# Layer norm sums on TensorE, its silu on ScalarE, and the third attention branch among the second group's heads

## The chip, the cores and the metric

The kernel runs on one core of one Trainium2 chip. The metric is the device time of one execution in microseconds (us), as the median of several runs. The engines named here are TensorE (PE: matmuls, and PEld for its weight loads), VectorE (DVE), ScalarE (ACT), GpSimd (POOL) and SyncE (SP), which issues the loads of the weights.

## The reference, cut to what matters

A trunk of two layers on 256 tokens of width 2048, in float32. Each layer is a mixer and a gated feed-forward part, each with an RMS norm ahead and a residual sum behind. Only the first layer's mixer is touched: a conv module and a sparse attention read the same input, and their outputs (1024 columns each) go through one output product.

```
def conformer_conv(u, conv_w, conv_b, ln_w, ln_b):
    a, g = split(u, 2)
    h = a * sigmoid(g)
    h = causal_depthwise_conv(h, conv_w, width=31) + conv_b      # 1024 channels
    mu  = mean(h, axis=-1)
    var = mean(square(h - mu), axis=-1)
    hn  = (h - mu) * rsqrt(var + EPS) * ln_w + ln_b
    return silu(hn)

def nsa_attention(q, k_cmp, v_cmp, k_slc, v_slc, k_win, v_win, gates):
    # 16 heads of 64, 4 key groups; three branches a head, each a masked softmax
    o_cmp = softmax(q @ k_cmp - slope * dist) @ v_cmp            # 15 compressed blocks
    o_slc = softmax(q @ k_sel - slope * dist) @ v_sel            # selected blocks
    o_win = softmax(q @ k_win - slope * dist) @ v_win            # window
    return gate0 * o_cmp + gate1 * o_slc + gate2 * o_win

def even_mixer(h, ...):
    u = h @ w_in                        # conv input, q, six key and value inputs, gates
    a_out = conformer_conv(u[conv part], ...)
    b_out = nsa_attention(u[the rest], ...)
    return concatenate([a_out, b_out]) @ w_out
```

## The kernel before

**Tiles.** Features lie on the 128 partitions and the 256 tokens along the free dimension. A float32 value is kept as a high and a low part (`xhl`, `mhl`: a tile of four features blocks by two parts by 256 tokens), and a product with a weight is three matmuls: high by high, low by high, high by low. A weight block comes by a DMA from SyncE's queue into `raw` (L167); ScalarE copies its high part `whi` (L178), and VectorE or GpSimd subtracts the low part `wlo` (L179). The tuple `lo_pool` says which: it is read in turn, and a 1 gives the block to GpSimd. The matmuls of L204 to L206 sum the three products in one PSUM tile `acc`; L229 to L231 do the same for the value inputs.

**Order.** `drive` (L237) takes a list of jobs, each a weight block's worth of output columns in four units, and a list of background steps; it spreads the steps over the units, up to the share `until` of them. A scheduler then sets each engine's order from these priorities; within an engine instructions start in order.

**The mixer's stages** (function `even`). The conv inputs come first (jobs 0 to 7). The conv has 31 taps per channel tile on VectorE (L408 to L411), 8 tiles in four pairs; the running sum of a pair lies in PSUM (`mx`), and the last tap writes the tile of `cy`. The taps are the background of jobs 2 to 7, of the key jobs 8 and 9, the value job, the gate job and the query jobs 12 and 13 of head group 0. Next come jobs 14 and 15 (queries of group 1) and 10 and 11 (the inputs that are compressed, `evac_c`, L529), with the layer norm as background: `ln_steps` (L421 to L479).

**The layer norm before.** GpSimd adds the eight tiles of `cy` to one (L432, L427, L428), TensorE takes the mean over channels with one matmul (L437), ScalarE copies it to SBUF, VectorE subtracts it from both halves of `cy` (L444), ScalarE squares them (L446), GpSimd adds the squares (L450, L427, L428). `inv_rms` (L133) has two matmuls of one column for the sum over partitions (L139), the inverse root on VectorE, a matmul that spreads it over the partitions (L150) and a copy (L152). The product with it is on GpSimd for one half and VectorE for the other (L459), scale and bias are eight VectorE instructions (L461), silu is a sigmoid on ScalarE (L468) and a product on GpSimd (L469), and then the halves are parted into `mhl` (L475 high, L476 low), which the output product's matmuls read.

**Output product and attention.** `out_jobs(0, 8)` multiplies the conv's eight tiles by the first half of `w_out`; its background is the compression of keys and values (`compress_steps`; its block sums are L628 on GpSimd), the heads of group 0 (`attn[0][0]`: scores, weigh, turn, values) and then group 0's third branch `attn[0][1]`. `out_jobs(8, 12)` needs group 0's output, and has group 1's heads and, behind them, its third branch `attn[1][1]` as background. `out_jobs(12, 16)` needs group 1's output. The third branch has six steps: `cmp_scores` (matmuls L842, copies L850, transposes L855, bias add L858, slope L861), `cmp_exp` (L867 to L869), `cmp_sum` (L874 to L886), `cmp_turn` (transposes L894, copy L897) and two `cmp_values` (matmuls L904, sum L914, and the split into `mhl`).

Of the kernel before, what the change touches and what calls it, by code (L numbers as in the profile page):

```python
# [10 lines left out]
F32 = mybir.dt.float32  # L11
# [57 lines left out]
class Net:  # L69
# [62 lines left out]

    def inv_rms(self, sums, n):  # L133


        nc = self.nc
        ps = self.mx()
        for tb in range(2):
            nc.tensor.matmul(ps[:, tb : tb + 1], sums[:, tb * 128 : tb * 128 + 128], self.ones[:, 0:1], start=True, stop=True)  # L139
        v = self.tile(self.tp, [128, 2], "rs_v", bufs=2)  # L140
        nc.vector.tensor_scalar(v, ps[:, 0:2], 1.0 / n, EPS, op0=ALU.mult, op1=ALU.add)
        tok = self.tile(self.tp, [128, 2], "rs_tok", bufs=2)
        self.rsqrt(tok, v, "rs")
        diag = self.t256("rs_diag", bufs=1)
        for tb in range(2):
            nc.vector.tensor_scalar(
                diag[:, tb * 128 : tb * 128 + 128], self.ca("ident"), tok[:, tb : tb + 1], None, op0=ALU.mult
            )
        pb = self.mx()
        nc.tensor.matmul(pb[:, :S], self.ones, diag, start=True, stop=True)  # L150
        bc = self.t256("rs_bc", bufs=2)
        nc.scalar.copy(bc, pb[:, :S])  # L152
        return tok, bc
# [155 lines left out]
    def norm_done(self):  # L309
        self.tok, self.bc = self.inv_rms(self.ssq, D)  # L310

# [48 lines left out]
    def even(self, xhl, start):  # L360
# [60 lines left out]
        def ln_steps():  # L421
            st = {}
            t4 = lambda tag, dt=F32: self.tile(cv, [128, 4, S], tag, dt)
            w, b = self.cb("lnw"), self.cb("lnb")

            def fold(t):
                nc.gpsimd.tensor_add(t[:, 0:2], t[:, 0:2], t[:, 2:4])  # L427
                nc.gpsimd.tensor_add(t[:, 0], t[:, 0], t[:, 1])  # L428

            def ysum():  # L430
                st["s"] = s = self.quarter("mhl1", (128, 4, S), F32)
                nc.gpsimd.tensor_add(s, cy[:, 0:4], cy[:, 4:8])  # L432
                fold(s)

            def mean():
                pm = self.mx()
                nc.tensor.matmul(pm[:, :S], self.mean1024, st["s"][:, 0], start=True, stop=True)  # L437
                m = self.tile(cv, [128, S], "l_m")
                nc.scalar.copy(m, pm[:, :S])
                st["m"] = m  # L440

            def center(h):
                y = cy[:, 4 * h : 4 * h + 4]
                nc.vector.tensor_sub(y, y, st["m"].unsqueeze(1).to_broadcast([128, 4, S]))  # L444
                q = st[h] = t4("l_q") if h else self.quarter("mhl0", (128, 4, S), F32)
                nc.scalar.activation(q, y, AF.Square)  # L446

            def sqsum():
                q = st[0]
                nc.gpsimd.tensor_add(q, q, st[1])  # L450
                fold(q)

            def var():
                _, st["r"] = self.inv_rms(st[0][:, 0], 1024)

            def out(h):
                y = cy[:, 4 * h : 4 * h + 4]
                eng = nc.vector if h else nc.gpsimd
                eng.tensor_mul(y, y, st["r"].unsqueeze(1).to_broadcast([128, 4, S]))  # L459
                for j in range(4 * h, 4 * h + 4):  # L460
                    nc.vector.tensor_scalar(  # L461
                        cy[:, j], cy[:, j], w[:, j : j + 1], b[:, j : j + 1], op0=ALU.mult, op1=ALU.add
                    )

            def silu(h):
                y = cy[:, 4 * h : 4 * h + 4]
                g = t4("l_q")
                nc.scalar.activation(g, y, AF.Sigmoid)  # L468
                nc.gpsimd.tensor_mul(y, y, g)  # L469

# [7 lines left out]
            two = lambda f: [lambda: f(0), lambda: f(1)]  # L478
            return [ysum, mean] + two(center) + [sqsum, var] + two(out) + two(silu) + two(parts)  # L479

# [46 lines left out]
        def evac_c(kv):  # L527
# [13 lines left out]
        self.raw_size = 2048  # L541
        self.lo_pool = (0, 1, 1)
        self.drive([job(1, evac_a(0))], [lambda: nc.sync.dma_start(self.cst_b, a["cst_b"])], until=0.25)
# [7 lines left out]
            + [job(12 + i, evac_q(0, i)) for i in range(2)],  # L551
            conv,
            until=0.98,
# [3 lines left out]
            [job(14 + i, evac_q(1, i)) for i in range(2)] + [job(10, evac_c(0)), job(11, evac_c(1))],  # L557
            [turn_gates] + ln_steps() + [self.lower_bound],
            until=0.8,
# [32 lines left out]
        heads = attn[0][0]  # L592
        mixed = []
        for i in range(max(len(comp), len(heads))):
            mixed += comp[i : i + 1] + heads[i : i + 1]
        self.drive(out_jobs(0, 8), mixed + attn[0][1] + attn[1][0][:5])
        self.drive(out_jobs(8, 12), attn[1][0][5:] + attn[1][1], until=0.8)
        self.lo_pool = (0,)
# [124 lines left out]
    def nsa(self, P, q4, kt, vt, gt, o):  # L723
# [107 lines left out]
        def cmp_scores():  # L831

            mem = self.quarter("xhl3", (128, 1280), F32)
            z = cs["z"] = mem[:, 0:256].rearrange("p (b h n) -> p b h n", b=2, h=8)
# [504 lines left out]
```

## Time and profile before

| what | value |
|---|---|
| median of 3 runs | 2456.01 us (2455.55 to 2456.85) |
| profiled execution, its own time | 2458.43 us |
| its span in the trace | 2456.2 us |
| TensorE busy | 2396.2 us (98%) |
| VectorE, ScalarE, GpSimd busy | 1543.1, 1171.6, 622.2 us |
| mean granted clock of TensorE | 0.989 of full speed |
| stage of the conv's taps, 62 to 192 us: TensorE, VectorE, GpSimd busy | 129.42, 123.56, 73.42 us of 130 |
| 440 us to the end: TensorE busy | 1999.22 us of 2016 |

The span is what the trace covers; the execution's own time is 2.2 us longer. A row on a wait names the engine and line that waited, then the engine, tile and line that ended the wait. The granted clock is a share of TensorE's full speed; 0.50 is the lower of its two levels (1.2 and 2.4 GHz). Stretches are in us from the span's start.

### The profile page before, as it was taken

How to read it: one execution, taken by the hardware profiler on the slowest of the kernel's cores; microseconds unless marked ns; L12 is line 12 of the kernel's file. 1: busy time of each engine (PE TensorE's matmuls, PEld its weight loads, DVE VectorE, ACT ScalarE, POOL GpSimd, SP SyncE). 2: the span in 40 equal slices, each digit the busy share in tenths (PEclk: the TensorE clock that was granted, in tenths of full speed). 3: DMA queues.
4: the chain of work that ended last, by engine and by line, in shares of the span. 5: the costliest groups of instructions: out<-in, count | busy, mean ns of one | idle time of the engine just before them, and what ended most of it. 6: DMA issues, size and time to landing. Idle time of an engine off the chain costs nothing.

```text
span 2456.2 us, 36598 instructions
## 1 busy us (share of the span) xinstructions
PE 2396.2 (98%) x14532; PEld 2114.6 (86%) x14532; DVE 1543.1 (63%) x2253; ACT 1171.6 (48%) x1728; POOL 622.2 (25%) x586
## 2 busy tenths in 40 slices
PE   7999898999999999999999999999999999999997
PEld 6999877888888888888888888888888888888886
DVE  7997556756555655557656766676655555555554
ACT  4344444645444544455544443355544444444554
POOL 5656522311111121113203223132111111121123
PEclk9999999999999999999999999999999999999998
DMA  5554422655555555555554444445555555555553
GB/s 204 185 169 163 159 72 69 215 189 187 188 187 187 186 179 194 188 183 187 191 180 164 155 155 155 151 158 188 185 187 188 186 188 188 183 191 189 188 183 125
DMA packets 62267, 427.89 MB, mean 174 GB/s; under 512 B 6928, under 2 KB 7056, under 8 KB 15248
## 3 DMA queue, kind: packets, MB, share of 16 engines
q1 hardware_dynamic: 61776, 425.04, 52.2%
q8 instruction: 114, 1.87, 0.3%
q10 hardware_dynamic: 320, 0.52, 0.1%
q14 instruction: 57, 0.47, 0.1%
HBM read 422.91 MB, written 2.10 MB: 173 GB/s over the span
## 4 chain that ended last, share of the span: by engine, by line
PE 94%; DVE 3%; POOL 1%; issue 1%; ACT 0%; DMA 0%; DVEq 0%; SPq 0%; POOLq 0%; ACTq 0%
PE acc L211 44%; PE acc L212 22%; PE acc L204 3%; PE acc L205 3%; PE acc L206 3%; PE acc L209 3%; PE acc L230 2%; PE acc L229 2%; PE acc L231 2%; PE acc L208 2%; PE mx L1071 1%; DVE wlo L179 1%; PE mx L643 1%; PE mx L745 1%; DVE a_z L788 0%
## 5 line engine op out<-in xcount | busy, mean ns | idle before, releaser
L179 DVE TENSOR_TENSOR wlo<-raw,whi 128x1024 fp32r<-128x1024 f32 x754 | 972.1, 1290 | 679.8 <-ACT whi L178 670.0
L178 ACT ACTIVATE whi<-raw 128x1024 fp32r<-128x1024 f32 (+1 forms) x809 | 843.6, 1043 | 915.1 <-PE acc L211 605.4
L211 PE MATMUL acc<-xhl,whi 128*128 128x512 f32 x3120 | 1089.4, 395 | 0.0
L212 PE MATMUL acc<-xhl,wlo 128*128 128x256 f32 x3120 | 844.3, 281 | 0.0
L211 PEld LDWEIGHTS acc<-xhl,whi 128*128 128x128 f32 x3120 | 573.1, 188 | 111.0
L212 PEld LDWEIGHTS acc<-xhl,wlo 128*128 128x128 f32 x3120 | 588.9, 189 | 25.0
L211 PE MATMUL acc<-mhl,whi 128*128 128x512 f32 x1500 | 520.5, 396 | 1.9 <-DVE mhl L120 1.8
L212 PE MATMUL acc<-mhl,wlo 128*128 128x256 f32 x1500 | 398.7, 281 | 0.0
L264 POOL TENSOR_TENSOR e_u<-e_s,rs_bc 128x256 f32<-128x256 f32 x192 | 148.6, 775 | 905.7 <-DVE e_s L257 867.8
L211 PEld LDWEIGHTS acc<-mhl,whi 128*128 128x128 f32 x1500 | 274.0, 188 | 53.5 <-DVE mhl L120 2.0
L212 PEld LDWEIGHTS acc<-mhl,wlo 128*128 128x128 f32 x1500 | 283.2, 189 | 15.5 <-DVE wlo L179 0.2
L278 POOL TENSOR_TENSOR x<-x,e_c 128x256 f32<-128x256 f32 x108 | 109.0, 1022 | 420.2 <-DVE x L277 420.2
L179 POOL TENSOR_TENSOR wlo<-raw,whi 128x1024 fp32r<-128x1024 f32 (+1 forms) x55 | 136.4, 2481 | 132.1 <-ACT whi L178 125.7
L204 PE MATMUL acc<-xhl,whi 128*128 128x256 f32 (+1 forms) x528 | 149.6, 289 | 8.6 <-ACT whi L178 8.6
L206 PE MATMUL acc<-xhl,wlo 128*128 128x256 f32 (+1 forms) x528 | 149.6, 289 | 6.6 <-DVE wlo L179 3.6
L205 PE MATMUL acc<-xhl,whi 128*128 128x256 f32 (+1 forms) x528 | 150.5, 288 | 3.7 <-DVE xhl L1199 3.7
L255 ACT COPY e_c<-acc 128x256 f32<-128x256 f32 x208 | 77.6, 373 | 156.0 <-PE acc L209 155.9
L257 DVE TENSOR_TENSOR e_s<-acc,e_c 128x256 f32<-128x256 f32 x208 | 87.3, 421 | 72.2 <-ACT e_c L255 70.2
L230 PE MATMUL acc<-wlo,xhl 128*128 128x512 f32 x288 | 114.0, 396 | 0.6 <-DVE wlo L179 0.6
L231 PE MATMUL acc<-whi,xhl 128*128 128x512 f32 x288 | 112.5, 391 | 0.0
L204 PEld LDWEIGHTS acc<-xhl,whi 128*128 128x128 f32 (+1 forms) x528 | 102.7, 195 | 8.9 <-ACT whi L178 8.6
L206 PEld LDWEIGHTS acc<-xhl,wlo 128*128 128x128 f32 (+1 forms) x528 | 102.0, 195 | 7.8 <-DVE wlo L179 4.1
(226 smaller groups left out, 2569.8 us busy)
## 6 DMA issues: line engine op xcount, KB each, us to landing
raw<-in_gu SPq DMA_DIRECT2D x176, 1024.0 KB, 5.0
raw<-in_dn SPq DMA_DIRECT2D x64, 1024.0 KB, 5.1
raw<-in_od_fq SPq DMA_DIRECT2D x32, 1024.0 KB, 5.0
raw<-in_od_ig SPq DMA_DIRECT2D x32, 1024.0 KB, 4.8
raw<-in_ev_in SPq DMA_DIRECT2D x30, 1024.0 KB, 5.0
raw<-in_dn SPq DMA_DIRECT2D x32, 768.0 KB, 4.4
raw<-in_od_out SPq DMA_DIRECT2D x16, 1024.0 KB, 5.0
raw<-in_ev_out SPq DMA_DIRECT2D x8, 1024.0 KB, 5.1
```

Source lines behind the costliest of these rows:

```text
L178: nc.scalar.activation(hi[:, :m], rs, AF.Copy)
L179: eng.tensor_sub(lo[:, :m], rs, hi[:, :m].bitcast(F32))
L204: nc.tensor.matmul(o[:, :S], h, a[:, 0, :], start=first, stop=False)
L205: nc.tensor.matmul(o[:, :S], h, a[:, 1, :], start=False, stop=False)
L206: nc.tensor.matmul(o[:, :S], l, a[:, 0, :], start=False, stop=end)
L211: nc.tensor.matmul(o, h, both, start=first, stop=False)
L212: nc.tensor.matmul(o[:, S:], l, a[:, 0, :], start=False, stop=False)
L230: nc.tensor.matmul(o, src(k)[:, 0, t], lo[:, i, :], start=False, stop=False)
L231: nc.tensor.matmul(o, src(k)[:, 1, t], hi[:, i, :], start=False, stop=(k == nkt - 1))
L257: nc.vector.tensor_add(s, ps[:, :S], c)
L264: self.nc.gpsimd.tensor_mul(u, s, self.bc)
L278: nc.gpsimd.tensor_add(x, x, c)
```

## The change

The layer norm's mean is summed by TensorE: eight matmuls, one for each tile of `cy`, add up in one PSUM tile, and VectorE reads the mean from there; the first six are background steps among the last twenty taps. `inv_rms` takes a list of tiles, for the layer norm the eight tiles of squares, which is two times eight matmuls of one column in place of GpSimd's sums and two matmuls; without the copy the broadcast stays in PSUM. VectorE multiplies both halves; one ScalarE activation (Silu, with scale and bias per channel) takes the place of scale, bias, sigmoid and product. The rest of the layer norm steps come ahead of the gates' transpose. During the conv `lo_pool` gives GpSimd three of four weight blocks instead of two of three. Group 0's third branch alternates with the first six steps of group 1's heads, group 1's with the rest of its heads; its scratch takes another buffer (`xhl1`).

```diff
-    def inv_rms(self, sums, n):
+    def inv_rms(self, sums, n, copy=True):
...
-            nc.tensor.matmul(ps[:, tb : tb + 1], sums[:, tb * 128 : tb * 128 + 128], self.ones[:, 0:1], start=True, stop=True)
+            for i, q in enumerate(sums):
+                nc.tensor.matmul(
+                    ps[:, tb : tb + 1],
+                    q[:, tb * 128 : tb * 128 + 128],
+                    self.ones[:, 0:1],
+                    start=(i == 0),
+                    stop=(i == len(sums) - 1),
+                )
...
+        if not copy:
+            return tok, pb[:, :S]
         bc = self.t256("rs_bc", bufs=2)
         nc.scalar.copy(bc, pb[:, :S])
...
-            def ysum():
-                st["s"] = s = self.quarter("mhl1", (128, 4, S), F32)
-                nc.gpsimd.tensor_add(s, cy[:, 0:4], cy[:, 4:8])
-                fold(s)
-
-            def mean():
-                pm = self.mx()
-                nc.tensor.matmul(pm[:, :S], self.mean1024, st["s"][:, 0], start=True, stop=True)
-                m = self.tile(cv, [128, S], "l_m")
-                nc.scalar.copy(m, pm[:, :S])
-                st["m"] = m
+            def mean(j0, j1):
+                if j0 == 0:
+                    st["m"] = self.mx()[:, :S]
+                for j in range(j0, j1):
+                    nc.tensor.matmul(st["m"], self.mean1024, cy[:, j], start=(j == 0), stop=(j == 7))
...
-            def sqsum():
-                q = st[0]
-                nc.gpsimd.tensor_add(q, q, st[1])
-                fold(q)
-
             def var():
-                _, st["r"] = self.inv_rms(st[0][:, 0], 1024)
+                _, st["r"] = self.inv_rms([st[j // 4][:, j % 4] for j in range(8)], 1024, copy=False)
 
             def out(h):
                 y = cy[:, 4 * h : 4 * h + 4]
-                eng = nc.vector if h else nc.gpsimd
-                eng.tensor_mul(y, y, st["r"].unsqueeze(1).to_broadcast([128, 4, S]))
+                nc.vector.tensor_mul(y, y, four(st["r"]))
                 for j in range(4 * h, 4 * h + 4):
-                    nc.vector.tensor_scalar(
-                        cy[:, j], cy[:, j], w[:, j : j + 1], b[:, j : j + 1], op0=ALU.mult, op1=ALU.add
-                    )
-
-            def silu(h):
-                y = cy[:, 4 * h : 4 * h + 4]
-                g = t4("l_q")
-                nc.scalar.activation(g, y, AF.Sigmoid)
-                nc.gpsimd.tensor_mul(y, y, g)
+                    nc.scalar.activation(cy[:, j], cy[:, j], AF.Silu, scale=w[:, j : j + 1], bias=b[:, j : j + 1])
...
-            return [ysum, mean] + two(center) + [sqsum, var] + two(out) + two(silu) + two(parts)
+            return [lambda: mean(0, 6)], [lambda: mean(6, 8)] + two(center) + [var] + two(out) + two(parts)
...
-        self.lo_pool = (0, 1, 1)
+        self.lo_pool = (0, 1, 1, 1)
+        ln_first, ln_rest = ln_steps()
...
-            conv,
+            conv[:-20] + ln_first + conv[-20:],
             until=0.98,
...
-            [turn_gates] + ln_steps() + [self.lower_bound],
+            ln_rest + [turn_gates, self.lower_bound],
...
-        self.drive(out_jobs(0, 8), mixed + attn[0][1] + attn[1][0][:5])
-        self.drive(out_jobs(8, 12), attn[1][0][5:] + attn[1][1], until=0.8)
+        third = [attn[P][1] for P in range(2)]
+        spread = lambda x, y: [st for i in range(max(len(x), len(y))) for st in x[i : i + 1] + y[i : i + 1]]
+        self.drive(out_jobs(0, 8), spread(comp, attn[0][0]) + spread(attn[1][0][:6], third[0]))
+        self.drive(out_jobs(8, 12), spread(attn[1][0][6:], third[1][:4]) + third[1][4:], until=0.85)
...
-            mem = self.quarter("xhl3", (128, 1280), F32)
+            mem = self.quarter(f"xhl{3 - 2 * P}", (128, 1280), F32)
```

Behind this stage each engine's order is the one before, and SyncE's loads come in the same order throughout. Line numbers of the changed kernel differ; where the order is shown, its matmuls of L204, L205 and L206 are L213, L214 and L215.

TensorE's order at the layer norm, before: the mean (L437) stands in job 15 (`acc_2258`, `acc_2259`), the variance (L139) in job 10 (`acc_2421`, `acc_2422`), the broadcast (L150) in job 11 (`acc_2559`).

```order
L206 MATMUL acc_2258<-xhl_28_146,wlo_2294 128x256
L437 MATMUL mx_2214<-mhl_248_2180,mean_8_82 128x256
L206 MATMUL acc_2259<-xhl_28_146,wlo_2294 128x256
...
L206 MATMUL acc_2421<-xhl_33_184,wlo_2492 128x256
L139 MATMUL mx_2354<-ones_80,mhl_259_2256 128x1 x2
L204 MATMUL acc_2422<-xhl_33_184,whi_2491 128x256
...
L204 MATMUL acc_2559<-xhl_10_87,whi_2562 128x256
L150 MATMUL mx_2376<-rs_diag_2373,ones_80 128x256
```

And in the changed kernel: the last two matmuls of the mean (L439) stand in job 14 (`acc_2123`, `acc_2124`), the variance (L140) in job 15, the broadcast (L157) between job 15 and job 10 (`acc_2432`).

```order
L215 MATMUL acc_2124<-xhl_28_146,wlo_2156 128x256
L439 MATMUL mx_1970<-cy_98,mean_8_82 128x256 x2
L213 MATMUL acc_2123<-xhl_33_184,whi_2187 128x256
...
L215 MATMUL acc_2259<-xhl_28_146,wlo_2291 128x256
L140 MATMUL mx_2318<-ones_80,mhl_257_2256 128x1 x4
L140 MATMUL mx_2318<-ones_80,mhl_251_2216 128x1 x4
L140 MATMUL mx_2318<-ones_80,mhl_257_2256 128x1 x4
...
L214 MATMUL acc_2259<-xhl_38_222,whi_2391 128x256
L157 MATMUL mx_2354<-rs_diag_2351,ones_80 128x256
L213 MATMUL acc_2432<-xhl_10_87,whi_2436 128x256
```

Each of the three stands about one job earlier; the broadcast has 1609 rows of TensorE's order ahead of it before and 1501 now.

TensorE's order at the end of group 1's third branch, before: values of the heads (L814), then the branch's scores, transposes and values, then the output's last quarter (`mhl_567`).

```order
L814 MATMUL mx_4231<-a_t_4184,vt_16_103 64x128
L842 MATMUL mx_4243<-mhl_256_2234,kcmp_109 128x256 x12
L855 MATMUL mx_4270<-cst_a_73,xhl_548_4241 128x128 x4
L894 MATMUL mx_4325<-cst_a_73,xhl_548_4241 128x128 x4
L904 MATMUL mx_4365<-xhl_548_4241,vbd_107 64x256 x4
L904 MATMUL mx_4379<-xhl_548_4241,vbd_107 64x256 x4
L204 MATMUL acc_4426<-mhl_567_4372,whi_4430 128x256
```

And in the changed kernel, where L840, L879 and L889 are the first transposes, the second transposes and the values, and L799 the heads' values.

```order
L840 MATMUL mx_3994<-cst_a_73,xhl_499_3965 128x128 x3
L215 MATMUL acc_4053<-mhl_475_3853,wlo_4057 128x256
...
L215 MATMUL acc_4260<-mhl_475_3853,wlo_4264 128x256
L879 MATMUL mx_4175<-cst_a_73,xhl_499_3965 128x128 x4
L782 MATMUL mx_4181<-cst_a_73,a_z_3860 128x128
...
L803 MATMUL mx_4325<-a_t_4301,vt_15_102 64x256
L889 MATMUL mx_4369<-xhl_499_3965,vbd_107 64x256 x4
...
L799 MATMUL mx_4325<-a_t_4312,vt_16_103 64x128
L889 MATMUL mx_4383<-xhl_499_3965,vbd_107 64x256 x4
L213 MATMUL acc_4430<-mhl_562_4376,whi_4434 128x256
```

The two sets of transposes, one behind the other before, have 91 rows between them now (rows 2349 and 2440 of the order); in group 0 it is 65 (2189 and 2254).

## Rows read from the trace of the kernel before

**Rows 1.** The page, first part: busy us of each engine (share of the span).

```profile
PE 2396.2 (98%) x14532; PEld 2114.6 (86%) x14532; DVE 1543.1 (63%) x2253; ACT 1171.6 (48%) x1728; POOL 622.2 (25%) x586
```

**Rows 2.** Stretches from:to, length, busy us by engine, granted clock, DMA share, GB/s.

```profile
238.00:262.00 24.00, 13.65 (x87) 12.34 (x85) 8.93 (x10) 7.24 (x8) 23.40 (x31) 0.79 0.31 99
...
342.00:360.00 18.00, 13.18 (x66) 9.10 (x66) 8.81 (x34) 6.83 (x22) 2.71 (x4) 0.72 0.20 61
360.00:400.00 40.00, 37.90 (x291) 32.32 (x292) 35.87 (x122) 23.38 (x66) 7.38 (x3) 1.00 0.33 101
400.00:421.00 21.00, 14.44 (x96) 10.65 (x93) 6.38 (x16) 4.47 (x11) 5.16 (x10) 0.76 0.02 10
```

**Rows 3.** TensorE's waits, 0 to 440 us: us in total, times, longest.

```profile
PE mx L894 <- DVE xhl L886: 9.6, 2, 5.5
...
PE acc L204 <- ACT mhl L475: 6.1, 2, 5.2
...
PE acc L206 <- POOL wlo L179: 3.6, 2, 3.1
...
PE acc L205 <- DVE mhl L476: 1.7, 2, 1.1
PE mx L904 <- ACT xhl L897: 1.5, 2, 0.7
```

**Rows 4.** Stretches again, behind the three longest waits.

```profile
250.00:259.00 9.00, 7.08 (x33) 6.79 (x34) 2.24 (x1) 1.72 (x2) 8.67 (x14) 0.53 0.35 118
349.00:358.00 9.00, 9.00 (x41) 6.25 (x38) 4.57 (x20) 4.13 (x16) 0.53 (x1) 0.53 0.01 3
411.00:420.00 9.00, 6.90 (x34) 4.65 (x35) 4.53 (x13) 2.08 (x5) 1.99 (x4) 0.56 0.00 0
```

**Rows 5.** The chain of waits: start us, us, what; about 355 and 359 us.

```profile
355.42 0.21 PE acc L205
...
358.75 0.12 PE acc L205
```

**Rows 6.** Timeline of TensorE at the mean: start us, us, what.

```profile
209.19 0.59 PE L437 MATMUL mx<-mhl,mean 128*128 128x256 f32 x2
...
209.73 0.28 PE L204 MATMUL acc<-xhl,whi 128*128 128x256 f32 x1
```

**Rows 7.** Timeline of TensorE at the variance.

```profile
223.77 0.50 PE L139 MATMUL mx<-ones,mhl 128*128 128x1 f32 x4
...
224.33 0.28 PE L205 MATMUL acc<-xhl,whi 128*128 128x256 f32 x1
```

**Rows 8.** The layer norm behind its broadcast: VectorE's timeline, then the chain.

```profile
232.37 3.43 DVE L459 TENSOR_TENSOR cy<-cy,rs_bc 128x1024 f32<-128x1024 f32 x1
235.84 3.73 DVE L461 TENSOR_SCALAR cy<-cy,cst_b 128x256 f32<-128x256 f32 x8
...
258.48 2.38 POOL cy L469
...
260.88 1.07 ACT mhl L475
...
261.97 1.29 DVE mhl L476
```

**Rows 9.** ScalarE by form, 200 to 440 us: xcount, busy us, mean ns.

```profile
L770 ACT ACT_TABLE_LOAD x2 | 2.6, 1283 | 2.1 <-DVE a_n L756 2.0
...
L119 ACT ACTIVATE mhl<-e_u,cst_b 128x256 fp32r<-128x256 f32 x4 | 2.0, 506 | 2.3 <-DVE e_u L375 2.3
```

**Rows 10.** VectorE's taps and centering by line: ns min/median/max, first and last start.

```profile
L411 DVE SCALAR_TENSOR_TENSOR mx<-cin,cst_b,mx x219: 467/479/490, 59.9 to 195.9; 128x256 f32<-128x256 f32 x110
...
L444 DVE TENSOR_TENSOR cy<-cy,l_m x2: 1209/1588/1968, 210.3 to 212.2; 128x1024 f32<-128x1024 f32 x2
```

**Rows 11.** The chain of waits through group 1's third branch.

```profile
406.87 0.44 DVE xhl L858
...
412.37 1.10 PE mx L894 x4
```

More of the change, by code (lines that the diff above doesn't have):

```diff
@@ L309, in norm_done @@
     def norm_done(self):
-        self.tok, self.bc = self.inv_rms(self.ssq, D)
+        self.tok, self.bc = self.inv_rms([self.ssq], D)
     def nw(self, i):
@@ L422, in ln_steps @@
             st = {}
-            t4 = lambda tag, dt=F32: self.tile(cv, [128, 4, S], tag, dt)
             w, b = self.cb("lnw"), self.cb("lnb")
-            def fold(t):
-                nc.gpsimd.tensor_add(t[:, 0:2], t[:, 0:2], t[:, 2:4])
-                nc.gpsimd.tensor_add(t[:, 0], t[:, 0], t[:, 1])
-            def ysum():
-                st["s"] = s = self.quarter("mhl1", (128, 4, S), F32)
-                nc.gpsimd.tensor_add(s, cy[:, 0:4], cy[:, 4:8])
-                fold(s)
-            def mean():
-                pm = self.mx()
-                nc.tensor.matmul(pm[:, :S], self.mean1024, st["s"][:, 0], start=True, stop=True)
-                m = self.tile(cv, [128, S], "l_m")
-                nc.scalar.copy(m, pm[:, :S])
-                st["m"] = m
+            four = lambda t: t.unsqueeze(1).to_broadcast([128, 4, S])
@@ L442, in center @@
+            def mean(j0, j1):
[3 more added lines that the diff above has]
+                    nc.tensor.matmul(st["m"], self.mean1024, cy[:, j], start=(j == 0), stop=(j == 7))
             def center(h):
                 y = cy[:, 4 * h : 4 * h + 4]
-                nc.vector.tensor_sub(y, y, st["m"].unsqueeze(1).to_broadcast([128, 4, S]))
-                q = st[h] = t4("l_q") if h else self.quarter("mhl0", (128, 4, S), F32)
+                nc.vector.tensor_sub(y, y, four(st["m"]))
+                q = st[h] = self.quarter(f"mhl{h}", (128, 4, S), F32)
@@ L592, in even @@
         heads = attn[0][0]
-        mixed = []
-        for i in range(max(len(comp), len(heads))):
-            mixed += comp[i : i + 1] + heads[i : i + 1]
-        self.drive(out_jobs(0, 8), mixed + attn[0][1] + attn[1][0][:5])
-        self.drive(out_jobs(8, 12), attn[1][0][5:] + attn[1][1], until=0.8)
+        third = [attn[P][1] for P in range(2)]
+        spread = lambda x, y: [st for i in range(max(len(x), len(y))) for st in x[i : i + 1] + y[i : i + 1]]
+        self.drive(out_jobs(0, 8), spread(comp, attn[0][0]) + spread(attn[1][0][:6], third[0]))
+        self.drive(out_jobs(8, 12), spread(attn[1][0][6:], third[1][:4]) + third[1][4:], until=0.85)
         self.lo_pool = (0,)
```

## The prediction

> **What bounds the kernel now.** I read the page's first part, then the span cut into stages, then TensorE's waits up to 440 us (where the stage that the change touches ends), then the granted clock around the longest of them, and last the chain of waits through the same places. TensorE is busy for 2396.2 of 2456.2 us [rows 1]: a change can gain only what TensorE still loses, which is time without work and time at the lower clock. Near the change the loss lies in three stretches [rows 2]: 238 to 262 us (13.65 us busy of 24), 342 to 360 (13.18 of 18) and 400 to 421 (14.44 of 21); in each the mean granted clock is 0.72 to 0.79, while 360 to 400, between them, has 37.90 of 40 at 1.00. Few waits fill them [rows 3]. In the first stretch TensorE waits for the layer norm's output: 6.1 us for ScalarE's high parts (L475), 1.7 for VectorE's low parts (L476), and 3.6 for a weight's low part that GpSimd makes between layer norm steps. In the other two it waits for the third attention branch: 9.6 us, in two waits, for the softmax that VectorE ends at L886, then 1.5 for the copy at L897. That is 6.1 + 1.7 + 3.6 = 11.4 and 9.6 + 1.5 = 11.1, 22.5 us together.
>
> Behind the longest wait of each stretch (5.2, 9.6 - 5.5 = 4.1, and 5.5 us) lies a time at the lower of TensorE's two clock levels: 250 to 259, 349 to 358 and 411 to 420 us have a granted clock of 0.53 to 0.56, and 7.08 + 9.00 + 6.90 = 22.98 us of busy time [rows 4]. The chain shows the price: the same matmul has a step of 0.21 us there and of 0.12 us behind it [rows 5]. So 0.09 / 0.21 = 43% of 22.98, 9.9 us, is lost to the clock: 3.0, 3.9 and 3.0 by stretch.
>
> **The change part by part.** *Mean on TensorE.* One matmul on a folded sum becomes eight on the conv's tiles. The one starts at 209.19 and the second weight matmul behind it at 209.73 [rows 6]; one step of 0.12 us would be there anyway, so it costs 0.54 - 0.12 = 0.42 us. Seven more are 7 x 0.42 = +2.9 us, all in TensorE's queue and so on the path.
>
> *Variance on TensorE.* Two matmuls of one column become sixteen. The two start at 223.77, the second weight matmul behind them at 224.33 [rows 7]: 0.56 - 0.12 = 0.44, or 0.22 each, and fourteen more are +3.1 us. Twelve of them now stand side by side, where nothing covers their weight loads; by the busy time of the pair, 0.50 us, fourteen are at most 3.5. Together the new matmuls are +6.0 us (0 where they fall into a wait, 6.5 at most).
>
> *Chain of the layer norm.* GpSimd loses all its sums and products, VectorE the eight scale and bias steps, ScalarE two copies. Before, the broadcast of the inverse deviation is there at 232.37, when VectorE starts its product; the steps of L461 end at 239.57, GpSimd ends the second half's product with the sigmoid at 260.86, and the last low part ends at 263.26 [rows 8]: 31 us. What is left of it after the broadcast is two products on VectorE (1.21 to 1.97 each, as the same shape at L444 [rows 10]), a table load of 1.28 and eight silus at the 0.50 of a 128x256 activation with scale [rows 9], two high parts of 1.07 and two low parts of 1.29: 2 x 1.6 + 1.28 + 8 x 0.5 + 2 x 1.07 + 2 x 1.29 = 13.2 us, even if nothing overlaps. The broadcast itself moves forward by about 108 places of TensorE's order, at 0.12 us some 13 us. So the output's parts are there about 18 + 13 = 31 us sooner, 6 of which the new matmuls take back, against waits of 7.8: both go. Eight silus and a table load now stand on ScalarE's queue ahead of a weight's copy, and GpSimd's low part of that weight stands behind the copy; this and the block sums (L628), still ahead of one low part on GpSimd, are late next. Of the 3.6 us behind GpSimd I leave 1.0 (between 0 and 3.6).
>
> *Its inputs.* The mean's matmuls stand in TensorE's queue ahead of weight matmuls, so a late conv tile now holds TensorE and all that is queued there. VectorE makes a quarter of the weights' low parts instead of a third during the conv, five fewer in the program, and the last conv tiles stand one query evacuation earlier in its order. I take 0.5 us (between 0 and 3).
>
> *Third branch.* Before, group 1's chain from the bias add (406.87) to the transposes (412.37) takes 5.50 us with nothing else on TensorE [rows 11]; the order has its scores, transposes and values one behind the other. Now 65 (group 0) and 91 (group 1) rows of TensorE's order stand between the two sets of transposes, at 0.12 us and more each 8 and 11 us of work. The chain's steps in turn queue behind the heads' steps on VectorE, which was busy for 35.87 of 40 us among them [rows 2], so 5.5 us may become 8 to 12. I take a rest of 1.5 us for the first group, 0.5 for the second and 0.5 for the last split ahead of the output's last quarter; the ends are 0 (covered) and 11.1 (as before).
>
> *Clock.* These rests are each under 2 us, smaller than the 4.1 to 5.5 behind which it fell. I keep 1.5 us for one such fall in part; the ends are 0 and 9.9.
>
> *Shared port, weighed.* VectorE's conv taps, with one operand in PSUM, stay within 467 to 490 ns over 219 instructions; L444, with both operands in SBUF, took 1.21 and 1.97 us [rows 10]. The Trainium skill (SBUF — State Buffer, section "SBUF: two separate sides") says that GpSimd and a VectorE instruction with two SBUF inputs hold their shared port pair as an exclusive lock, and the loser waits for the whole instruction. The rows agree in kind; how long a blocked low part waits, they don't show. By the rule GpSimd's larger share speaks against the change: four low parts of VectorE in the last part of the conv, each blocked for a GpSimd instruction of 2.4 us, would bring the last conv tiles up to 9.6 us later, less what the fewer low parts save; at the upper end of that term, 3 us, the forecast would be some 2.5 us higher. The sum keeps the rows.
>
> *Sum.* Waits -22.5, clock -9.9, matmuls +6.0, rests 1.0 + 0.5 + 1.5 + 0.5 + 0.5 = +4.0, clock that stays +1.5: -20.9 us. The profiled execution took 2458.43 us, 2.2 over its span and 2.4 over the median of the runs, 2456.01. So 2437.5 for such an execution, and 2435 beside the median.
>
> **The rivals.**
> *All of it goes.* No rest anywhere: -22.5 - 9.9 + 6.0 = -26.4, which is 2430. For it: the layer norm has some 17 us to spare. Against: with VectorE at 90% the heads are likely to keep small waits.
>
> *Only the layer norm gains.* The branch is spread, but VectorE is so full that TensorE still meets the transposes early, for about as long as before: -11.4 - 3.0 + 1.5 + 6.0 = -6.9, which is 2449. For it: 35.87 of 40 us. Against: there were no matmuls at all between the pieces in group 1, and now there are 11 us of them.
>
> *Slower.* One mechanism: TensorE takes its queue in order, and the spread branch puts transposes and values at four places among the heads where a full VectorE or ScalarE can be behind; before there were two. A wait of 5 us there brings 3.0 to 3.9 us of lower clock with it [rows 3, 4], so 8.5 a place. With two such places the branch is as before and the time 2449; three give 2458, four 2466. It decides from the third place with a wait of over 4 us. For it: each wait of that size in this trace brought the lower clock. Against: the work that stands in front of each place.
>
> That the change doesn't do what it says has no chance of its own: the order shows every move.
>
> **How the numbers follow.** The forecast's own case (2431 to 2441) 0.57; all of it goes 0.14; only the layer norm 0.17; the four places 0.08; half of the third branch's gain, 2441 to 2446, 0.04. The range of 2426 to 2450 leaves out the places' case and the ends of the others. 0.2%, 4.9 us, is about what a measurement of this kernel can tell from no change. The same: 0.04 of the layer norm's case and 0.03 of the places' case, 0.07; slower: the other 0.05 of the places' case; faster: 0.88.
>
> **What would show it.** In the changed trace the waits for the layer norm's high and low parts should be gone, those for the third branch's softmax under 2 us each, and the granted clock 1.0 from 200 to 440 us. The mean's eight matmuls should start right behind weight matmuls, at some 0.42 us each, and the variance's sixteen take about 3.5 us together. The broadcast should come by 222 us and the last low part by 240. I am wrong if TensorE waits at the mean's matmuls for conv tiles, if a wait of over 4 us stands among the heads, or if the lower clock appears in a new place.

## The result and the profile after

The changed kernel takes 2433.05 us (median of 4 runs, 2431.20 to 2434.38), the kernel before 2456.43; the ratio is 0.9903 (95% interval 0.9890 to 0.9915), 23.4 us less. Timed again beside the experiments it took 2431.38 (ratio 0.9896, 0.9883 to 0.9910). The forecast was 2435 in a range of 2426 to 2450. The profiled execution took 2434.38 us with a span of 2432.6; that of the second timing has a span of 2429.4. The profiled execution of the kernel before took 2458.43 us, 2.0 over the median of its runs, so that differences between the traces come out somewhat larger than those of the medians.

TensorE's waits from 60 to 440 us in the changed kernel (us in total, times, longest):

```profile
PE mx L879 <- DVE xhl L871: 2.0, 1, 2.0
PE acc L215 <- DVE wlo L188: 1.6, 1, 1.6
PE mx L889 <- ACT xhl L882: 0.7, 1, 0.7
```

These are all. Of the waits of [rows 3] none is left for the layer norm, and of the third branch's only the first group's, 2.0 and 0.7 us (L879 and L889 are what L894 and L904 were). The stretches of [rows 2] in the changed kernel's trace, and two short ones behind them (length, busy us by engine, granted clock, DMA share, GB/s):

```profile
238.00:262.00 24.00, 24.00 (x194) 22.76 (x194) 16.11 (x44) 15.75 (x41) 21.31 (x30) 1.00 0.47 154
...
342.00:360.00 18.00, 15.81 (x99) 12.12 (x100) 11.91 (x52) 6.78 (x23) 0.00 (x0) 0.81 0.19 59
360.00:400.00 40.00, 40.00 (x330) 35.45 (x329) 26.49 (x69) 18.97 (x41) 15.02 (x16) 1.00 0.35 106
400.00:421.00 21.00, 21.00 (x169) 20.59 (x168) 20.91 (x37) 17.04 (x32) 9.42 (x10) 1.00 0.61 207
216.00:222.00 6.00, 6.00 (x40) 6.00 (x40) 2.58 (x14) 1.06 (x1) 0.16 (x1) 0.72 0.38 156
344.00:351.00 7.00, 6.27 (x29) 3.96 (x30) 5.71 (x25) 4.22 (x16) 0.00 (x0) 0.51 0.26 81
```

The first and the last of the three stretches are full now. Two lower clocks remain, at 344 to 351 us behind the remaining wait, and at 216 to 222, where TensorE is busy throughout. To see the whole stage at once I cut it at the same two matmuls in each trace, the first of the value job and the broadcast of the next norm. Before, and then the changed kernel in its two profiled executions (length, TensorE's busy us, clock, DMA share, GB/s):

```profile
141.50:463.10 321.60, 295.98 (x2190) 0.95 0.41 134
```

```profile
142.40:439.60 297.20, 292.76 (x2230) 0.98 0.44 145
```

```profile
142.70:436.20 293.50, 289.06 (x2229) 1.00 0.44 147
```

Idle time fell from 25.62 to 4.44 us in both, 21.2 us less. The trace shows a matmul of 256 columns as 0.28 us where its step is 0.12, so each wait begins with some 0.16 us that count as busy; with twelve waits fewer (15 before, 3 now) that is another 1.9 us of waiting, some 23.1 in all. Busy time fell by 3.2 us in the first execution and by 6.9 in the second, although there are 21 matmuls more, which cost about 6.0 us. The second has no lower clock in this stage at all, so the clock cost the kernel before, in its profiled execution, an estimated 6.9 + 6.0 - 1.9 = 11.0 us, and in the first execution 292.76 - 289.06 = 3.7 us of such a cost are still there. Outside this stage the traces differ by about 1 us.

The new matmuls in TensorE's timeline: the last two of the mean, then twelve of the variance's sixteen, each with the weight matmuls behind them. The trace has two records for each of these float32 matmuls, hence x4 and x24.

```profile
200.62 1.02 PE L439 MATMUL mx<-cy,mean 128*128 128x256 f32 x4
201.29 0.47 PE L213 MATMUL acc<-xhl,whi 128*128 128x256 f32 x1
201.60 0.28 PE L214 MATMUL acc<-xhl,whi 128*128 128x256 f32 x1
...
213.88 2.74 PE L140 MATMUL mx<-ones,mhl 128*128 128x1 f32 x24
216.47 0.36 PE L213 MATMUL acc<-xhl,whi 128*128 128x256 f32 x1
216.68 0.28 PE L214 MATMUL acc<-xhl,whi 128*128 128x256 f32 x1
```

The two of the mean cost 201.60 - 200.62 - 0.12 = 0.86 us, 0.43 each, and the twelve 216.68 - 213.88 - 0.12 = 2.68, 0.22 each, as worked out ahead from [rows 6, 7]. VectorE's center steps (L443, now from PSUM) and products (L452), ScalarE's silus and the low parts (ns min/median/max, first and last start):

```profile
L443 DVE TENSOR_TENSOR cy<-cy,mx x2: 1214/1218/1222, 201.7 to 202.8; 128x1024 f32<-128x1024 f32 x2
...
L452 DVE TENSOR_TENSOR cy<-cy,mx x2: 1205/1206/1207, 224.8 to 225.9; 128x1024 f32<-128x1024 f32 x2
...
L454 ACT ACTIVATE cy<-cy,cst_b x8: 586/587/601, 226.7 to 231.1; 128x256 f32<-128x256 f32 x8
...
L461 DVE TENSOR_TENSOR mhl<-cy,mhl x2: 1218/1222/1226, 232.7 to 235.1; 128x1024 fp32r<-128x1024 f32 x2
```

The last low part ends at 236.4 us, 27 us earlier than in [rows 8], and 11 us ahead of the output product's first matmul on it, at 247.2.

### The profile page after: what moved, and what is told of

It is laid out like the page before. It is cut to its first block, busy times and chain, and to the rows that moved or that the text cites. A ratio compares the mean times of both kernels' runs of the same rounds, so it can differ in the third digit from the quotient of the medians.

```text
span 2432.6 us, 36663 instructions
## 1 busy us (share of the span) xinstructions
PE 2390.5 (98%) x14574; PEld 2113.4 (87%) x14574; DVE 1526.7 (63%) x2241; ACT 1173.7 (48%) x1733; POOL 611.1 (25%) x582
## 4 chain that ended last, share of the span: by engine, by line
PE 97%; DVE 2%; DMA 0%; issue 0%; ACT 0%; DVEq 0%; SPq 0%; POOL 0%; POOLq 0%; ACTq 0%
PE acc L220 44%; PE acc L221 22%; PE acc L213 4%; PE acc L215 4%; PE acc L214 4%; PE acc L218 3%; PE acc L238 3%; PE acc L239 3%; PE acc L240 3%; PE acc L217 2%; PE mx L1056 1%; PE mx L730 1%; PE mx L628 1%; PE mx L1021 0%; DVE wlo L188 0%; PE mx L1064 0%
## 5 line engine op out<-in xcount | busy, mean ns | idle before, releaser
L188 DVE TENSOR_TENSOR wlo<-raw,whi 128x1024 fp32r<-128x1024 f32 (+1 forms) x749 | 960.6, 1283 | 684.2 <-ACT whi L187 674.4
L188 POOL TENSOR_TENSOR wlo<-raw,whi 128x1024 fp32r<-128x1024 f32 (+1 forms) x60 | 146.1, 2437 | 150.4 <-ACT whi L187 145.8
L213 PE MATMUL acc<-xhl,whi 128*128 128x256 f32 (+1 forms) x528 | 149.1, 288 | 8.8 <-ACT whi L187 8.8
L214 PE MATMUL acc<-xhl,whi 128*128 128x256 f32 (+1 forms) x528 | 149.6, 287 | 3.9 <-DVE xhl L1184 3.9
L215 PE MATMUL acc<-xhl,wlo 128*128 128x256 f32 (+1 forms) x528 | 149.2, 289 | 4.0 <-DVE wlo L188 4.0
L240 PE MATMUL acc<-whi,xhl 128*128 128x512 f32 x288 | 112.5, 391 | 0.0
L213 PEld LDWEIGHTS acc<-xhl,whi 128*128 128x128 f32 (+1 forms) x528 | 102.2, 194 | 9.1 <-ACT whi L187 8.8
L238 PE MATMUL acc<-whi,xhl 128*128 128x512 f32 x288 | 108.3, 394 | 0.0
```

Source lines behind the costliest of these rows:

```text
L188: eng.tensor_sub(lo[:, :m], rs, hi[:, :m].bitcast(F32))
L213: nc.tensor.matmul(o[:, :S], h, a[:, 0, :], start=first, stop=False)
L214: nc.tensor.matmul(o[:, :S], h, a[:, 1, :], start=False, stop=False)
L215: nc.tensor.matmul(o[:, :S], l, a[:, 0, :], start=False, stop=end)
L238: nc.tensor.matmul(o, src(k)[:, 0, t], hi[:, i, :], start=(k == 0), stop=False)
L240: nc.tensor.matmul(o, src(k)[:, 1, t], hi[:, i, :], start=False, stop=(k == nkt - 1))
```

## The experiments

My theory ahead of them: the change has two parts that are worth what their own waits held, with the lower clock behind these as a cost of its own and the new matmuls as a price on TensorE. The rivals were that one part carries the gain, that the clock is no cost of its own, and that details (the silu's form, the tuple of low parts) carry it. All ratios are to the kernel before, with 95% intervals.

| run | median us | ratio | interval |
|---|---|---|---|
| ln_only | 2448.96 | 0.9969 | 0.9957 to 0.9980 |
| third_only | 2442.15 | 0.9944 | 0.9931 to 0.9956 |
| before_fill | 2455.26 | 0.9992 | 0.9984 to 1.0001 |
| after_again | 2431.38 | 0.9896 | 0.9883 to 0.9910 |
| var_fold | 2432.40 | 0.9906 | 0.9893 to 0.9920 |
| both_fold | 2431.81 | 0.9897 | 0.9882 to 0.9912 |
| old_silu | 2438.19 | 0.9924 | 0.9912 to 0.9937 |
| lo_23 | 2430.21 | 0.9893 | 0.9880 to 0.9907 |
| lo_dve | 2436.48 | 0.9919 | 0.9906 to 0.9933 |
| phase | 2441.12 | 0.9935 | 0.9921 to 0.9948 |
| both_phase | 2435.47 | 0.9910 | 0.9897 to 0.9924 |

**The two parts apart: ln_only and third_only.** The first is the changed kernel with the old drives behind the layer norm, the second the old kernel with the new drives:

```diff
 ln_only, against the changed kernel
...
-        self.drive(out_jobs(0, 8), spread(comp, attn[0][0]) + spread(attn[1][0][:6], third[0]))
-        self.drive(out_jobs(8, 12), spread(attn[1][0][6:], third[1][:4]) + third[1][4:], until=0.85)
...
+        self.drive(out_jobs(0, 8), mixed + attn[0][1] + attn[1][0][:5])
+        self.drive(out_jobs(8, 12), attn[1][0][5:] + attn[1][1], until=0.8)
...
-            mem = self.quarter(f"xhl{3 - 2 * P}", (128, 1280), F32)
+            mem = self.quarter("xhl3", (128, 1280), F32)
```

> The changed kernel with the third branch and its heads in the order of before: the layer norm's edits and the low parts' tuple alone. Theory (the two parts are separate, each worth what its own waits held): the waits of 11.4 us for the layer norm and their 3.0 us of lower clock go, 6.0 us of matmuls come, and the 1.5 us of lower clock that the changed kernel shows behind the variance's matmuls stay, so about 7 us under before, near 2449; the trace still has the two waits of 4 to 5.5 us for the branch's softmax, each with the lower clock behind it. Rival (the layer norm carries the gain, the branch only follows it): most of the 23 us, under 2440.

> The kernel before with only the third branch's steps spread among the heads. Theory: the two waits for the softmax (9.6 us) and 6.9 us of lower clock go, save about 2.7 us of wait and 3 us of lower clock at the first group as in the changed kernel: 10 to 12 us under before, near 2445, and the sum of this gain and that of the layer norm's part alone is the whole gain within 4 us. Rival (the late layer norm output holds back everything behind it, so that a spread branch finds the heads later and waits as before): within 4 us of before.

They gained 7.6 and 14.4 us by their medians, together 22.0 against 23.4 to 25.4 for both: the parts add up within the measurement. TensorE's waits in ln_only, and the stretches of its two lower clocks:

```profile
PE mx L880 <- DVE xhl L872: 9.7, 2, 5.5
...
PE mx L890 <- ACT xhl L883: 1.5, 2, 0.7
```

```profile
336.00:347.00 11.00, 8.74 (x45) 5.66 (x45) 5.80 (x25) 4.38 (x16) 0.52 (x1) 0.69 0.22 71
...
398.00:409.00 11.00, 7.92 (x49) 6.00 (x50) 4.88 (x13) 2.08 (x5) 3.91 (x8) 0.69 0.01 1
```

The branch's waits are what they were in [rows 3], to 0.1 us. In third_only it is the layer norm's that stay:

```profile
PE acc L204 <- ACT mhl L475: 6.2, 2, 5.2
PE acc L206 <- POOL wlo L179: 3.6, 2, 3.1
PE mx L892 <- DVE xhl L884: 2.0, 1, 2.0
PE acc L205 <- DVE mhl L476: 1.7, 2, 1.1
```

The stage cut as above, in ln_only and then in third_only:

```profile
141.60:450.40 308.80, 293.60 (x2226) 0.98 0.42 140
```

```profile
141.10:444.00 302.90, 287.96 (x2189) 0.98 0.43 143
```

TensorE is idle for 15.20 and 14.94 us, so 10.4 and 10.7 us of waiting go apart and 21.2 together. The waits add up, and neither part holds up the other: both rivals fall. The lengths of the stage do not add up: 12.8 and 18.7 us less are 31.5, against 24.4 and 28.1 for both. What differs is the clock: behind the same two waits of the branch ln_only has 0.69 over 11 us, where the profiled execution of the kernel before has 0.53 from 347 to 358 and from 408 to 419 us. third_only gained 2 to 4 us more than I expected; behind its remaining wait of 2.0 us the clock stayed at 1.00, where I had counted 3 us.

**The clock's own price: before_fill.** The kernel before, with work for TensorE in one wait:

```diff
         def cmp_turn():
             pp = cs["p"]
+            if P == 1:
+                fl = self.mx()
+                for i in range(9):
+                    nc.tensor.matmul(fl[:, :S], ident, cs["t"][:, 256:512], start=(i == 0), stop=(i == 8))
```

> The kernel before with nine matmuls of 256 columns, whose sum nobody reads, in the second group's wait for the softmax: TensorE works for 9 x 0.43 = 3.9 of the 5.5 us in which it waited. Theory (the lower clock behind a wait is a cost of its own, 3.0 us by the steps of 0.21 and 0.12): the wait shrinks to under 2 us, the granted clock at 408 to 419 us is 1.00 and the time 2 to 4 us under before; the layer norm's and the first group's stretches stay. Rival (the clock is no cost of its own, the time goes with the wait's end, which other engines set): the same time as before within 1 us.

The whole time, 1.6 us less, does not tell the theory from the rival: the interval includes 1. The stage does. The stretch of [rows 4] that had 0.56, in this kernel's trace:

```profile
408.00:419.00 11.00, 8.38 (x52) 6.47 (x53) 4.44 (x12) 1.82 (x5) 3.52 (x7) 1.00 0.00 0
```

No stretch from 361 us to the next norm has a lower clock here. The first of the branch's scores in this group and the next norm's broadcast, before and then in this run:

```profile
401.12 1.69 PE L842 MATMUL mx<-mhl,kcmp 64*128 64x256 f32 x12
...
463.06 0.59 PE L150 MATMUL mx<-rs_diag,ones 128*128 128x256 f32 x2
```

```profile
402.94 1.68 PE L842 MATMUL mx<-mhl,kcmp 64*128 64x256 f32 x12
...
462.38 0.59 PE L150 MATMUL mx<-rs_diag,ones 128*128 128x256 f32 x2
```

Between the two it is 61.9 us before and 59.4 here: 2.5 us less with the same chain and 3.9 us more of matmuls. So that stretch of lower clock cost 2.5 us by itself, and idle time and its clock have to be counted apart. The profiled execution lost it again at the layer norm, where its granted clock is low from 243 to 261 us; before it was from 248 to 259.

**The price of the new matmuls: var_fold and both_fold.** GpSimd adds the squares, and in both_fold six of the conv's tiles as well:

```diff
             def var():
-                _, st["r"] = self.inv_rms([st[j // 4][:, j % 4] for j in range(8)], 1024, copy=False)
+                q = st[0]
+                nc.gpsimd.tensor_add(q, q, st[1])
+                nc.gpsimd.tensor_add(q[:, 0:2], q[:, 0:2], q[:, 2:4])
+                nc.gpsimd.tensor_add(q[:, 0], q[:, 0], q[:, 1])
+                _, st["r"] = self.inv_rms([q[:, 0]], 1024, copy=False)
...
 both_fold, in mean()
...
+                    nc.gpsimd.tensor_add(s[:, 0:2], cy[:, 0:2], cy[:, 2:4])
+                    nc.gpsimd.tensor_add(s[:, 0:2], s[:, 0:2], cy[:, 4:6])
...
+                nc.gpsimd.tensor_add(s[:, 0], s[:, 0], s[:, 1])
+                for i, x in enumerate((s[:, 0], cy[:, 6], cy[:, 7])):
+                    nc.tensor.matmul(st["m"], self.mean1024, x, start=(i == 0), stop=(i == 2))
```

> The changed kernel with the squares added on GpSimd as before (three instructions), so that two matmuls of one column stand in place of sixteen. Theory (the matmuls are paid on TensorE, 0.23 us each, and the run of one-column matmuls brought the lower clock with no wait; GpSimd's extra time is hidden, since the halves are ready 20 us ahead of their use): 3.1 + 1.5 = 4.6 us under the changed kernel, near 2428.5, and the granted clock is 1.00 from 192 to 240 us. Rival 1 (the clock fell for another reason): the lower clock stays, 3 us gained. Rival 2 (GpSimd's sums bring the layer norm's waits back): slower than the changed kernel by 3 us or more.

> The changed kernel with the squares added on GpSimd (two matmuls of one column) and six of the conv's eight tiles added on GpSimd too (three matmuls for the mean): 19 matmuls fewer on TensorE. Theory (the new matmuls are a cost of 0.43 and 0.23 us each on TensorE with nothing to show for it, as long as the halves come in time): 5 x 0.43 + 14 x 0.23 = 5.4 us less, and 1.5 us of clock behind the variance, with 1 to 2 us of new waits behind GpSimd as in the kernel with the squares alone: 3 to 5 us under the changed kernel, near 2429. Rival (VectorE and GpSimd pay: GpSimd's adds hold up VectorE's instructions on SBUF and its own weights): no gain, within 1.5 us of the changed kernel or above it.

(The 20 us of slack in these texts is 11: the output's first matmul stands at 247.2 us, not behind 257.) Neither is faster than the changed kernel beyond the measurement, and for var_fold none of the three outcomes of its text came: no gain, no loss of 3 us, and the same new waits as in both_fold. In both_fold's trace the layer norm comes in time, and other waits have come, one of them with the lower clock behind it:

```profile
PE mx L794 <- DVE a_t L797: 1.3, 1, 1.3
...
PE acc L215 <- POOL wlo L188: 0.7, 1, 0.7
PE acc L215 <- DVE wlo L188: 0.5, 1, 0.5
PE mx L157 <- DVE rs_diag L153: 0.5, 1, 0.5
```

```profile
276.00:283.00 7.00, 6.82 (x32) 6.83 (x33) 0.59 (x3) 0.00 (x0) 0.95 (x1) 0.51 0.83 307
```

Its stage, from the value job to the next norm, takes 293.1 us, as against 293.6 for the execution of the changed kernel without lower clock: 5.4 us of matmuls saved, and some 1.6 us of waits (6.0 us idle against 4.4) and an estimated 2.9 us of clock paid for it. The rival's outcome holds, by waits among the heads and not by the layer norm. In var_fold the granted clock from 216 to 222 us is 1.00 as expected; but so it is in the changed kernel's second profile, so this run does not show that the one-column matmuls lower the clock.

**The silu's form: old_silu.**

```diff
-                    nc.scalar.activation(cy[:, j], cy[:, j], AF.Silu, scale=w[:, j : j + 1], bias=b[:, j : j + 1])
+                    nc.vector.tensor_scalar(
+                        cy[:, j], cy[:, j], w[:, j : j + 1], b[:, j : j + 1], op0=ALU.mult, op1=ALU.add
+                    )
+            def silu(h):
+                y = cy[:, 4 * h : 4 * h + 4]
+                g = self.tile(cv, [128, 4, S], "l_q", F32)
+                nc.scalar.activation(g, y, AF.Sigmoid)
+                nc.gpsimd.tensor_mul(y, y, g)
...
```

> The changed kernel with scale and bias on VectorE, sigmoid on ScalarE and the product on GpSimd as before; the sums stay on TensorE. Theory (the layer norm gains by starting early and ending without GpSimd's sums; in the changed kernel its halves are parted by 236.3 us and first used after 257, some 20 us to spare, so the silu's shorter form is not needed): the parting comes 8 to 12 us later and still in time, no wait for the high parts, the time within 3 us of the changed kernel, with one wait of up to 3 us for a low part that GpSimd makes behind the products. Rival (the silu on ScalarE is what takes the layer norm off the path, GpSimd's products being behind its weights and block sums): the wait for the high parts is back with 3 us or more, and the lower clock behind it; 5 us or more above the changed kernel.

It is 6.8 us slower than the changed kernel beside it, and both texts missed why. The halves are parted in time (high parts by 240 us, first use at 249.3), so no wait for the high parts is back: the rival's time came, its mechanism did not. But VectorE, which has 4 us of instructions more, is late for its weights:

```profile
PE acc L215 <- DVE wlo L188: 3.1, 3, 1.4
PE mx L887 <- DVE xhl L879: 2.0, 1, 2.0
PE mx L790 <- DVE a_n L749: 1.2, 1, 1.2
PE mx L897 <- ACT xhl L890: 0.7, 1, 0.7
```

That is about 3 us more of waits. One of them, 0.7 us, ends at 239.96 us with a low part of VectorE that takes 3.41 us instead of 1.21, beside one of the products that GpSimd has back:

```profile
236.49 3.41 DVE L188 TENSOR_TENSOR wlo<-raw,whi 128x1024 fp32r<-128x1024 f32 x1
```

```profile
235.45 3.37 POOL L462 TENSOR_TENSOR cy<-cy,l_q 128x1024 f32<-128x1024 f32 x1
```

Some 3 us of lower clock, at 216 and at 349 us, make up most of the rest in the profiled execution. How much of the 6.8 us belongs to the silu and how much to a clock that varies by itself stays open.

Together with the folds this says what the layer norm's gain does not need. With most of the sums back on GpSimd (both_fold), and with the silu's old form (old_silu), the halves still come in time and no wait for them is back. Whether they would with both, so that the earlier start and the smaller edits alone are left, no run shows.

**The low parts' engines: lo_23, lo_dve, phase, both_phase.** One line each: `(0, 1, 1)` during the conv (lo_23), `self.lo_pool = (0,)` (lo_dve) or `(1, 0)` (phase; in both_phase with both folds) ahead of the output product. What led to the last three is VectorE's timeline at the remaining wait in the changed kernel, and GpSimd's beside it:

```profile
339.17 1.99 DVE L762 TENSOR_SCALAR a_s<-a_s 128x8 f32<-128x8 f32 x1
```

```profile
338.72 2.41 POOL L188 TENSOR_TENSOR wlo<-raw,whi 128x1024 fp32r<-128x1024 f32 x1
```

Eight elements a partition take 1.99 us and end at 341.16, with GpSimd's low part at 341.13.

> The changed kernel with two of three instead of three of four low parts on GpSimd during the conv, as before. Theory (the mean's matmuls have 4 us and more of slack to the conv's tiles, so the tuple is no part of the gain): within 1.5 us of the changed kernel, no wait at the mean's matmuls. Rival (with the mean's matmuls in TensorE's queue the conv needs VectorE to be relieved): TensorE waits for the conv's tiles at the mean, 2 to 6 us above the changed kernel.

> The changed kernel with all weights' low parts on VectorE from the output product's start on (it was every second one on GpSimd). In the changed trace a VectorE instruction on 128x8 elements (L762) takes 1.99 us, from 339.17 to 341.16, beside GpSimd's low part of 338.72 to 341.13, and TensorE then waits 1.98 us at the first group's transposes, with the lower clock behind it. Theory (GpSimd's low part holds VectorE up, and that wait comes from it): the 1.99 goes back to about 0.19, the wait falls under 0.5 us, the lower clock behind it goes too, 3 to 5 us under the changed kernel, near 2429. Rival (VectorE is full among the heads, and 1.2 us more for each weight is paid at every score): new waits of 2 to 4 us for VectorE, the same time or up to 5 us above the changed kernel.

> The changed kernel with the tuple for the low parts turned from (0, 1) to (1, 0) from the output product on, so that VectorE and GpSimd swap their weights. In the changed kernel's traces TensorE waits 1.97 us each time for the first group's transposes, and a VectorE instruction on 128x8 elements lasts 1.99 us beside a low part on GpSimd. Theory (it is this one low part on GpSimd, by where it falls): with the same number of low parts on each engine the long instruction goes, and the wait with it, 2 us and in part the lower clock behind it, 2 to 4 us under the changed kernel. Rival (as with all low parts on VectorE, where 1.22 us of low part stood in the chain instead and the wait rose to 3.8): the wait stays at 2 us or more, the same time as the changed kernel or up to 3 us above it.

> The kernel with both folds on GpSimd (19 matmuls fewer on TensorE) and the swapped tuple together. The folds saved 3.4 us of the stage's time but for a wait of 1.3 us at a head's transposes with the lower clock behind it. Theory (that wait, for a VectorE copy, hangs on where the low parts fall too): without it and without the wait at the first group, 3 to 6 us under the changed kernel, near 2427. Rival (each such order finds another wait in heads where VectorE is full): within 2 us of the changed kernel.

lo_23 takes as long as the changed kernel, and TensorE waits for no conv tile: the tuple is no part of the gain. lo_dve and phase are slower than it, by 3 to 5 and by 8 to 10 us. That is the rival's outcome for lo_dve; for phase it is worse than the rival, which had up to 3 us. A small instruction that lasts as long as GpSimd's low part shows again, but no run took it away and the wait with it. In lo_dve, with no low part on GpSimd there, the same instruction (L763) is short, but the wait is longer; and in phase another small one of the chain meets GpSimd's next low part (345.26 to 347.97), and TensorE waits 4.9 us:

```profile
339.00 0.16 DVE L763 TENSOR_SCALAR a_s<-a_s 128x8 f32<-128x8 f32 x1
```

```profile
PE mx L880 <- DVE xhl L872: 3.8, 1, 3.8
```

```profile
346.03 1.97 DVE L869 TENSOR_SCALAR cp_s<-cp_s 128x16 f32<-128x16 f32 x1
```

```profile
PE mx L880 <- DVE xhl L872: 4.9, 1, 4.9
PE mx L783 <- DVE a_z L774: 2.3, 1, 2.3
```

In lo_dve two low parts of 1.2 us stand among VectorE's instructions of the chain instead. The Trainium skill (SBUF — State Buffer, section "SBUF: two separate sides") has the lock end with the other engine's instruction. These rows agree: 341.16 against 341.13, and 348.00 against 347.97. The page names VectorE instructions with two SBUF inputs or in a two-port mode; these two have one input, and no run shows their mode. In phase the waits are some 4 us more than in the changed kernel, and lower clock, at 254 to 258 and at 346 to 357 us among others, makes up most of the rest. both_phase is slower than both_fold by 3.7 us, with the same wait of 4.9, and 2 to 4 us slower than the changed kernel, which neither the theory nor the rival of its text had. None of these is a version that beats the changed kernel.

## Why the prediction was right

**The waits.** 22.5 us were to go and 4.0 to stay, 18.5 less; the stage shows some 23.1 less. The layer norm's 11.4 us went whole, save one wait of 1.6 for a low part where I had 1.0; ln_only and third_only show that each part takes its own waits. The layer norm's chain came as sized: its broadcast starts 7.3 us earlier (223.8 for 231.1), where 13 less 6 were forecast. The branch kept 2.0 + 0.7 us in the first group (I had 1.5) and nothing in the second (0.5). This is the mis-sized term: beside the 1.9 us that the rows on waits don't hold, I had left out two waits among group 1's heads, 2.1 us together, that went with the spread branch (third_only has neither, ln_only has 0.9 and 0.7 us). In the kernel before:

```profile
PE mx L797 <- DVE a_n L756: 1.2, 1, 1.2
...
PE acc L204 <- DVE x L273: 0.9, 1, 0.9
```

**The matmuls.** 0.42 and 0.22 us each were forecast, 0.43 and 0.22 measured, +6.0 us. That they are a real price, and that GpSimd could not take it back, both_fold shows.

**The clock.** 9.9 us by the step of 0.21 against 0.12; the stage gives about 11.0, and before_fill 2.5 for the third stretch, for which I had 3.0. What stays was forecast as 1.5 us and is 3.7 or nothing, by execution, with the same waits: no single figure would have been right.

**The sum** came out 23.4 us under before (25.4 in the second timing) for 21 forecast. In the traces the waits gave 4.6 us more than forecast and the clock 1.1 more, and 2.2 more of it stayed in the first execution: 3.5 us, which is the stage's 24.4 less the 20.9 of the sum. The broadcast came at 223.8 us for "by 222", the last low part at 236.4 for "by 240". One of the signs of being wrong did appear: in the first profiled execution the lower clock is in a new place, 216 to 222 us, behind no wait, which the prediction had no term for. By the step of 0.21 against 0.12 it is an estimated 1.5 us.

**The rivals.** "Only the layer norm gains" put 2449 to its part alone, and ln_only measured 2448.96; but the branch's part worked. "Slower" needed a third place with a wait of over 4 us. No such place came here. Its mechanism shows in phase, in one place: a wait of 4.9 us and one of 2.3, with a granted clock of about half from 346 to 357 us, 8 to 10 us above the changed kernel, but still 16.5 under the kernel before. The weighed rule on the shared port cost the conv nothing that could be measured, as lo_23 shows. At the first group the instruction of 1.99 us stands in the chain ahead of the 2.0 us wait in both executions; that the wait comes from it is argued, not shown.

## What to carry to other kernels

Price a wait of the busiest engine together with the lower clock behind it, and list all waits of the stage, the small ones too: an order that lets the busiest engine do other work takes these along. The two parts' waits, in different stretches, added up here, so each could be forecast, and tried, alone. Where the busiest engine is 98% busy, a small change of order on an engine that is nearly full beside it (VectorE, 35.87 of 40 us before) moves waits about: put each variant on the chip, compare stages between the same two instructions, and count idle time and lower clock apart. The lengths alone mislead: the eight executions of the changed kernel lie between 2430.03 and 2434.38 us, and its stage took 297.2 and 293.6 us with the same 4.44 us of idle time.

## What the hardware showed that I had not expected

The same program has the lower clock at a place in one execution and not in another. Behind the same wait of 2.0 us the changed kernel's first profile has a granted clock of 0.51 from 344 to 351 us, and its second has 1.00:

```profile
216.00:222.00 6.00, 6.00 (x52) 6.00 (x52) 3.31 (x15) 1.23 (x2) 1.06 (x1) 1.00 0.37 152
344.00:351.00 7.00, 7.00 (x56) 5.30 (x53) 6.02 (x28) 5.36 (x21) 0.00 (x0) 1.00 0.24 77
```

At 216 to 222 us the first has 0.72 although TensorE waited for nothing; what it had done before it fell were the twelve one-column matmuls. The clock fell at this place in lo_dve, old_silu and phase too, and did not in ln_only, after_again and lo_23, with the same sixteen matmuls. It did not in the three kernels of this order without them (var_fold, both_fold, both_phase), which is too few to call it shown.

In the chain the 24 records of one column take 2.57 us, 0.107 each. The Trainium skill (TensorE: Matmul & The Clock Gate, section "LDWEIGHTS (loading the stationary operand)") gives a load of weights as its columns / 1.2 in ns, by which 128 columns are an estimated 106.7 ns. The step of 0.107 us agrees; the records of these loads last 0.192 us each and overlap. So such a run seems to cost its weight loads.

On ScalarE a silu with scale and bias takes 587 ns where a copy of the same shape with a scale took 506 [rows 9]. The table load takes 1.28 us, and the first silu starts where it ends, at 226.71 us.
